# A decoder block on one core: the first down group in seven products, its stores and factors moved, and weights at the moving operands' place in every block

## The chip, the cores and the metric

The kernel runs on one core of a Trainium2 chip. A core has five engines that run at the same time and wait for each other through semaphores: TensorE (PE; its weight loads are shown apart as PEld), VectorE (DVE), ScalarE (ACT), GpSimd (POOL) and SyncE (SP). Transfers between the chip's memory and the core run on DMA queues, which SP and POOL fill here. The metric is the device time of one execution, in microseconds (us), median of three runs.

## The reference

What is computed is one decoder block on 512 tokens of width 2048: a norm, a combined input projection, two kinds of attention, an output projection with residual, then a feed-forward part and a last norm. The change touches the feed-forward part:

```python
    hn2 = rmsnorm(h, norm2_g[l])
    h = h + (jax.nn.silu(hn2 @ w_gate[l]) * (hn2 @ w_up[l])) @ w_down[l]
return rmsnorm(h, final_g)
```

`w_gate` and `w_up` are 2048 x 5632, `w_down` is 5632 x 2048, all float32. The result must have float32 quality.

## The kernel before

**Three matmuls for one.** A float32 operand is split in two parts, a high one (`h`, rounded to TensorE's fast format, by ACT) and a low one (`l`, the rest, by DVE). A product is then three matmuls, high by high, high by low, low by high: `mm` (lines 1238 to 1241). For the weights the split is made as the kernel runs: ACT writes `wh` (line 143), DVE writes `wl` (line 146), for 512 columns at a time, which the text calls a half product's weights; `Twin` (lines 166 and 170) does it for two sets of 256. A list of such jobs is worked off three ahead of TensorE, through five buffers each of `wh` and `wl`.

**A place for weights.** `wsplit(even)` takes the weights' columns in a padded tile from column 32 where `even` is true and from column 16 else. The moving operands (`ah`, `al`, the terms of `hn2`) always start at column 32. So `even` means that weights lie in the moving operands' place; the text calls such a job "placed".

**The feed-forward part.** The hidden width of 5632 is worked off in 44 blocks `f` of 128. A block's gate and up values are four products (two weights, two halves of the contraction) by two token halves. They are computed as seven products of sums (a Strassen scheme), P1 to P7, each of 2 half products of 12 matmuls with 256 columns, so a block has 168. The sums of weights are made by DVE in place in the loaded tile `raw` (`comb`, line 819; `prep`, line 843), or, in the order `ORDER1`, one of them by an accumulating load on POOL's queue (`fetch`, line 823). `ORDER0` is block 0's order, `ORDER1` that of block 1 and of blocks with f % 4 of 3 and 0 above 4, `ORDER` that of the others.

**The down product** takes four blocks at a time, a group. For groups 1 to 9 it, too, has seven products: `down7` works on 56 pairs (output block k, product name), each of 6 matmuls, sorted into a first single one ahead of the last product of block f = 8, 12, ..., then 27 twins of two behind it, and a last single one in the next block. Its moving operands are sums of the silu values, made by `hidden_terms`, and its results are staged by ACT and added to `kept_sums` in memory by accumulating DMA writes on POOL's queue (line 1161). Group 0 (blocks 0 to 3) has eight products: `down`, 16 jobs of 24 matmuls with weights of their own (`wdn`, tile `rawd`), interleaved with block 4's later products; its 16 results are stored plainly (line 1338), after zeros were stored where no result of it falls (line 1365). Group 10 is the kernel's end and not touched.

**The residual.** The feed-forward's input `hs` (16 tiles of 128 x 512) leaves the core to make room: `put_away` stores it through POOL's queue (line 1357), eight tiles from block 1 on, eight from block 2 on, and at the last one opens the pool in which group work has its tiles. It comes back in blocks 5, 6, 9, 10, 13, 14, 17, 18 (`add_residual`), scaled by `inv`.

**The factors.** `inv` and `r2` come from the second norm. In block 0 each is spread over 512 columns by four matmuls (`Spread`, line 279; each is two passes) and copied to a buffer by ACT (line 282).

**Order of work.** Each engine has one queue, in the order in which the program issues. `later(n, f)` puts a piece of work n half products further back in that order; it makes no engine wait by itself. SP's queue issues weight loads as buffers come free, five `raw` tiles of 512 KB. POOL's queue issues the fetches, the stores and the accumulating writes, with at most eight in flight.

Of the kernel before, what the change touches and what calls it, by code (L numbers as in the profile page):

```python
# [23 lines left out]
PH = 4  # L24
# [18 lines left out]
def plan():  # L43

    p = [("c", u) for u in range(8)]
    n = 0
    for name in ("ks", "kw", "vs", "vw"):
        for half in range(2):
            p.append(("in", name, 0, half))
            for _ in range(W1_AFTER[name][half]):  # L50
                p.append(("w1", n))
                n += 1
    for j in range(NH):
        if j == 4:
# [12 lines left out]
    return p  # L67
# [7 lines left out]
def block_kernel(ctx: ExitStack, tc: tile.TileContext, xt, wst, wdn, smalls, wg, w2c, bias, ident_in, out):  # L75
# [710 lines left out]

    dn_loads = deque((0, nb) for nb in range(KB))
    dn = {}

    def load_dn():  # L790
        if dn_loads:
            k = dn_loads.popleft()
            dn[k] = wp.tile([128, 512], F32, tag="rawd", name="rawd", bufs=2)
            sp.dma_start(dn[k], wdn[k[0], k[1]])

    fin = []
# [14 lines left out]
    def quad_jobs(f, names):  # L811
# [59 lines left out]
    def dn_job(p, nb):  # L871
        return Job(lambda: dn[p, nb], post=load_dn)

# [37 lines left out]
    for f in range(FB):  # L911
        qj = quad_jobs(f, order(f))
        p = f // PH - 1
        nb = 0
        for i, name in enumerate(order(f)):
            seq = sorted(((k, n) for k in range(8) for n in DTIME), key=lambda x: 7 * x[0] + DTIME[x[1]])
            if name == "P3" and f > PH and f % PH == 0:
                downs(p, seq[:1], True)
            sched.append(("q", f, name))
            jobs += qj[2 * i:2 * i + 2]  # L920
            if name == "P3" and f > PH and f % PH == 0:
# [13 lines left out]
    state["total"] = len(jobs)  # L935
    load_dn()
    load_dn()

# [8 lines left out]
    def close_attention():  # L947
# [16 lines left out]
        def close():  # L964
# [8 lines left out]
            for _ in range(2):  # L973
                ffn.tile([128, S], F32, tag="ft", name="ft", bufs=2)
            rest["hsp"] = ExitStack()
# [41 lines left out]
    def ft(name="ft"):  # L1017
        return ffn.tile([128, S], F32, tag="ft", name=name, bufs=2)

    sacc = ft("sacc")  # L1020
# [87 lines left out]
    banks["P5"] = ps.tile([128, 512], F32, tag="o", name="P5")  # L1108
    dbanks = {}
# [31 lines left out]
    def down7(p, k, name, wh, wl):  # L1141

        if not roles:
            seed = ps.tile([128, 512], F32, tag="misc", name="pd")
            pe.matmul(seed[:, :256], ones, sm[:, :1].to_broadcast([128, 256]), start=True, stop=True)
            roles.append((banks["P3"], banks["P4"], seed, dbanks[1]))
            roles.append((banks["P1"], banks["P5"], banks["P7"], banks["P6"]))
# [36 lines left out]
    def hidden_terms(f):  # L1184

        i = (f - 1) % 2
        x3 = st["x3"]
        hl = [[a[:, 12:16, :].rearrange("p t (i c) -> p t i c", c=256)[:, :, i, :] for a in (ah, al)],
              [a.rearrange("p (t i c) -> p t i c", i=2, c=256)[:, :, i, :] for a in x3]]

# [6 lines left out]
        if f % PH in (1, 2):  # L1197
            top = held[f - 1]
            t = st["pool"].tile([128, 1, 256], F32, tag="s2", name="t1", bufs=2)

            def s1():
                dve.tensor_tensor(t[:, 0, :], top[:, LO], top[:, HI], op=OP.subtract)
                hi(1, 2, 3, top[:, None, LO])

            def s2():
                lo(1, 2, 3, top[:, None, LO])
                hi(0, 2, 3, t)
# [15 lines left out]
        def s2():  # L1223
            dve.scalar_tensor_tensor(t24[:, 0, :], t3[:, 0, :], -1.0, top[:, LO], op0=OP.mult, op1=OP.subtract)
            lo(0, 0, 2, botv)
            hi(0, 3, 4, t3)

        def s3():
            dve.scalar_tensor_tensor(t24[:, 1, :], t24[:, 0, :], -1.0, bot[:, LO], op0=OP.mult, op1=OP.subtract)
            lo(0, 3, 4, t3)  # L1230
            hi(1, 0, 2, t24)
# [11 lines left out]
    def finish(f, g, u, c):  # L1243
        whole = u
        g, u = g[:, c], u[:, c]
        h, l = ah[:, 12 + f % PH, c], al[:, 12 + f % PH, c]
        wait = 0 if f == FB - 1 else 1 if f < 8 or f % PH else 2

# [17 lines left out]
        later(n, up)  # L1266
        if f < PH or f > FB - PH:
            later(n + 1, lambda: dve.scalar_tensor_tensor(l, u, -1.0, h.bitcast(F32), op0=OP.mult, op1=OP.subtract))
# [9 lines left out]
    def after(f, name):  # L1278
# [43 lines left out]

    def down(ph, nb):
        n = nb % 3
        if n not in dbanks:
            dbanks[n] = banks["P3"] if not n else (ps.tile([128, 512], F32, tag="t", name="pd", bufs=2) if n == 1 else
                                                ps.tile([128, 512], F32, tag="misc", name="pd"))
        p = dbanks[n]
        h, l = next_half()
        for c in (LO, HI):  # L1330
            for i in range(PH):
                mm(p[:, c], h[:, 128 * i:128 * i + 128], l[:, 128 * i:128 * i + 128], ah[:, 12 + i, c],
                   al[:, 12 + i, c], i == 0, i == PH - 1)

        def add():
            t = st["pool"].tile([128, 2, 256], F32, tag="stga", name="stg", bufs=3)
            act.activation(t, p.rearrange("p (t c) -> p t c", c=256), AF.Copy, scale=1.0 if nb < 8 else -1.0)
            pool_e.dma_start(mem_at(nb), t)

        later(1, add)  # L1340

    def mem_at(nb):
# [13 lines left out]
    def put_away(nb):  # L1356
        pool_e.dma_start(kept_hs[nb], hs[:, nb, :])
        if nb == KB - 1:
            rest["hsp"].close()
            st["dnp"] = ExitStack()  # L1360
            pool = st["pool"] = st["dnp"].enter_context(tc.tile_pool(name="dnp", bufs=1))
            zero = pool.tile([128, 256], F32, tag="s2", name="zero", bufs=2)
            pool_e.memset(zero, 0.0)
            for k in range(8):
                pool_e.dma_start(kept_sums[k][:, 2, :], zero)
            st["x3"] = [placed(pool, 3 * S, at, name="x3" + x) for x, at in (("h", MH), ("l", ML))]
            for name, x, n in (("P2", 0, 0), ("P3", 0, 1), ("P5", 0, 2), ("P7", 0, 3), ("P6", 1, 0), ("P4", 1, 1), ("P1", 1, 2)):
                parts[name] = tuple((b[:, S * n:S * n + S] if x else a[:, 12 + n, :]).rearrange("p (i c) -> p i c", c=256)
# [10 lines left out]
    for kind, a, b in sched:  # L1379
        if kind == "d":  # L1380
            down(a, b)
            continue
        if kind == "s":
# [19 lines left out]
        if PH < f <= FB - PH and name == order(f)[2]:  # L1403
            for i, s in enumerate(hidden_terms(f)):
# [7 lines left out]
        if f == 0:  # L1412
# [5 lines left out]
            if name == "P6":  # L1418
                st["inv"] = st["inv"]()
                act.activation(st["rs2"].rs[:, 7, :1], ones[:, :1], AF.Silu)  # L1420
# [163 lines left out]
```

## Time and profile before

| | us |
|---|---|
| median of 3 runs | 2143.21 |
| lowest, highest | 2142.64, 2144.26 |
| the profiled execution | 2147.43 |
| its span | 2145.6 |
| granted TensorE clock, mean over it | 0.997 |

The profiled execution is one run with the hardware profiler on. Its span goes from the first to the last instruction; 1.8 us lie around it. The page's rows give busy time and counts by engine, then groups of instructions by line. Matmuls overlap, so their rows' durations (277 ns) are not their distance; the distance is read from the start times, or from a stretch's length by the number of matmuls that start in it. The feed-forward part's products run from 836.0 to 2085.6 us of the span.

### The profile page before, as it was taken

The page shows a single profiled execution, that of the slowest core. Times are in us where ns is not written, and L with a number is a line of the kernel's source. Part 1 is how long each engine was busy: PE and PEld are TensorE (multiplying, and loading weights), DVE is VectorE, ACT ScalarE, POOL GpSimd, SP SyncE. Part 2 cuts the span into 40 slices and gives each one's busy share as a digit, 9 for nine tenths or more (in the row PEclk, how much of TensorE's full clock was granted, in tenths as well). Part 3 has the DMA queues.
Part 4 walks back from the last instruction along what each step waited for, and adds up shares of the span by engine and source line. Part 5 has one row for each costly group of instructions (what it writes and reads, how often), then busy time and mean ns, then how long its engine had stood idle before and what let it go on. Part 6 is the DMA issues. An engine that isn't in the chain of part 4 may idle for free.

```text
span 2145.6 us, 41296 instructions
## 1 busy us (share of the span) xinstructions
PE 2128.1 (99%) x15346; PEld 1988.0 (93%) x15346; DVE 1629.4 (76%) x3460; ACT 1241.6 (58%) x2973; POOL 321.9 (15%) x378
## 2 busy tenths in 40 slices
PE   9999999999999999999999999999999999999997
PEld 7888888888888888999999999999999999999997
DVE  6755656366657678856989898898989898988885
ACT  6544444344445256444675858585767667675856
POOL 0000000000000001211131313131212213030323
PEclk9999999999999999999999999999999999999998
DMA  7442222322234334545596969775766758594982
GB/s 237 147 141 81 82 82 69 101 81 72 65 106 155 99 99 128 177 153 148 145 230 142 213 154 210 171 188 139 184 161 158 184 141 187 139 216 118 208 245 89
DMA packets 124347, 313.67 MB, mean 146 GB/s; under 512 B 13424, under 2 KB 35568, under 8 KB 124144
## 3 DMA queue, kind: packets, MB, share of 16 engines
q1 hardware_dynamic: 77104, 236.49, 34.9%
q0 software_dynamic: 46896, 74.47, 19.6%
q8 instruction: 120, 1.97, 0.4%
q14 instruction: 83, 0.68, 0.1%
q10 hardware_dynamic: 144, 0.07, 0.0%
HBM read 245.96 MB, written 65.01 MB: 145 GB/s over the span
## 4 chain that ended last, share of the span: by engine, by line
PE 96%; DMA 1%; DVE 1%; ACT 1%; issue 0%; SPq 0%; POOL 0%; DVEq 0%; ACTq 0%; POOLq 0%
PE P L1241 17%; PE P L1240 17%; PE P L1239 17%; PE pp L197 7%; PE pp L199 7%; PE pp L198 7%; PE pab L199 3%; PE pab L197 3%; PE pab L198 3%; PE pd L1239 2%; PE pd L1241 2%; PE pd L1240 2%; DMA raw<-in_wst_dram 1%; PE pt L568 1%; PE po L198 1%; PE pl L198 1%
## 5 line engine op out<-in xcount | busy, mean ns | idle before, releaser
L143 ACT ACTIVATE wh<-raw 128x512 fp32r<-128x512 f32 x888 | 532.7, 625 | 295.0 <-DVE raw L819 113.6
L146 DVE TENSOR_TENSOR wl<-raw,wh 128x512 fp32r<-128x512 f32 x888 | 599.3, 686 | 111.0 <-ACT wh L143 106.9
L1241 PE MATMUL P<-ah,wl 128*128 128x256 f32 x1536 | 426.1, 277 | 0.1
L1239 PE MATMUL P<-ah,wh 128*128 128x256 f32 x1536 | 425.2, 277 | 0.0
L1240 PE MATMUL P<-al,wh 128*128 128x256 f32 x1536 | 425.1, 277 | 0.0
L1241 PEld LDWEIGHTS P<-ah,wl 128*128 128x128 f32 x1536 | 288.3, 188 | 1.3 <-DVE wl L146 1.1
L1240 PEld LDWEIGHTS P<-al,wh 128*128 128x128 f32 x1536 | 288.4, 188 | 0.0
L1239 PEld LDWEIGHTS P<-ah,wh 128*128 128x128 f32 x1536 | 288.2, 188 | 0.0
L197 PE MATMUL pp<-ah,wh 128*128 128x512 f32 x640 | 260.5, 407 | 0.0
L199 PE MATMUL pp<-ah,wl 128*128 128x512 f32 x640 | 251.0, 392 | 0.0
L198 PE MATMUL pp<-al,wh 128*128 128x512 f32 x640 | 250.2, 391 | 0.0
L1161 POOL DMA_DIRECT2D sums<-stg x216 | 188.1, 927 | 312.0 <-ACT P L1155 150.0
L819 DVE TENSOR_TENSOR raw<-raw 128x512 f32<-128x512 f32 x270 | 185.7, 688 | 5.6 <-DMA raw<-in_wst_dram 2.0
L170 DVE TENSOR_TENSOR wl<-raw,wh 128x256 fp32r<-128x256 f32 x432 | 167.9, 420 | 27.3 <-ACT wh L166 25.8
L166 ACT ACTIVATE wh<-raw 128x256 fp32r<-128x256 f32 x432 | 159.2, 409 | 4.6 <-DVE raw L898 4.6
L199 PEld LDWEIGHTS pp<-ah,wl 128*128 128x128 f32 x640 | 120.2, 188 | 28.2 <-DVE wl L146 0.4
L197 PEld LDWEIGHTS pp<-ah,wh 128*128 128x128 f32 x640 | 120.5, 188 | 20.0 <-DVE tmp L369 0.5
L198 PEld LDWEIGHTS pp<-al,wh 128*128 128x128 f32 x640 | 120.6, 189 | 19.5
L555 ACT ACTIVATE e<-e,st 128x512 f32<-128x512 f32 (+1 forms) x96 | 53.7, 560 | 124.3 <-DVE st L549 124.3
L707 POOL TENSOR_TENSOR acc<-acc,osq 128x512 f32<-128x512 f32 x14 | 18.1, 1294 | 580.3 <-ACT osq L706 580.3
L1155 ACT ACTIVATE stg<-P 128x256 f32<-128x256 f32 x252 | 95.6, 381 | 12.7 <-PE P L1241 3.3
L197 PE MATMUL pab<-ah,wh 128*128 128x512 f32 x256 | 100.3, 392 | 0.0
(335 smaller groups left out, 5545.0 us busy)
## 6 DMA issues: line engine op xcount, KB each, us to landing
raw<-in_wst_dram SPq DMA_DIRECT2D x382, 512.0 KB, 4.2
sums<-stg POOLq DMA_DIRECT2D x160, 256.0 KB, 6.7
raw<-in_wst_dram POOLq DMA_DIRECT2D x42, 256.0 KB, 4.5
sums<-stg POOLq DMA_DIRECT2D x72, 128.0 KB, 6.3
bias<-in_bias_dram SPq DMA_DIRECT2D x16, 320.0 KB, 3.0
xc<-in_xt_dram SPq DMA_DIRECT2D x16, 256.0 KB, 3.5
rawd<-in_wdn_dram SPq DMA_DIRECT2D x16, 256.0 KB, 2.8
hs<-in_xt_dram SPq DMA_DIRECT2D x16, 256.0 KB, 5.7
```

Of the source, the lines that this page charges most:

```text
L143: act.activation(self.h, self.src(), AF.Copy)
L146: dve.tensor_tensor(self.l, self.src(), self.h.bitcast(F32), op=OP.subtract)
L166: act.activation(h, src(), AF.Copy)
L170: dve.tensor_tensor(l, src(), h.bitcast(F32), op=OP.subtract)
L197: pe.matmul(o, wh, mh, start=start, stop=False)
L198: pe.matmul(o, wh, ml, start=False, stop=False)
L199: pe.matmul(o, wl, mh, start=False, stop=stop)
L819: return lambda: dve.tensor_tensor(o(), o(), x(), op=OP.add)
L1161: return lambda s=sums[x]: pool_e.dma_start(kept_sums[k][:, q:q + n, :], s, accum_op=OP.add)
L1239: pe.matmul(o, wh, mh, start=start, stop=False, skip_group_check=True)
L1240: pe.matmul(o, wh, ml, start=False, stop=False, skip_group_check=True)
L1241: pe.matmul(o, wl, mh, start=False, stop=stop, skip_group_check=True)
```

## The change

It changes four things.

1. Group 0 is computed by seven products, too: its `downs` are scheduled in block 4 as the other groups' are in theirs, `down`, `dn_job`, `load_dn` and the separate weight loads go, and `hidden_terms` also runs for blocks 1 to 4. Its results are written to `kept_sums` plainly instead of accumulating, and the zeros are no longer stored. Blocks 0 to 3 keep their silu products (`held`) in two new buffers `early`, one `ft` buffer and one of the group pool. As the group pool is not open in blocks 1 and 2, the operand of P1 moves from the pool's tile to `ah`, that of P7 the other way, and a scratch tile becomes the idle PSUM bank of P3.
2. Block 1 makes its sums on DVE as `ORDER` blocks do (in the order of products of `ORDER1`); its two fetches on POOL's queue go. All 16 residual stores are issued from block 1's P1 on, in steps of 8/5 half products.
3. In block 0, `r2`'s four matmuls and copy come first; `inv`'s copy is put five half products further back.
4. The first job of every block but block 0 is placed (before: odd blocks and block 2), and so are two of the 27 twins of each group, n = 19 and n = 37, beside the first single one, which was placed already.

```diff
-        if f > PH and f % PH == 0:
+        if f and f % PH == 0:
             p += [("dn", f // PH - 1, k) for k in range(8)]
...
-            elif order(f) == ORDER1:
+            elif order(f) == ORDER1 and f > 1:
...
-        r["P1", 0].even = f == 2 or f % 2 == 1
+        r["P1", 0].even = f > 0
...
-            if name == "P3" and f > PH and f % PH == 0:
+            if name == "P3" and f and f % PH == 0:
                 for n in range(1, len(seq) - 1, 2):
-                    downs(p, seq[n:n + 2])
-            if name == "P1" and f > PH + 1 and f % PH == 1:
+                    downs(p, seq[n:n + 2], n in (19, 37))
+            if name == "P1" and f > PH and f % PH == 1:
                 downs(p, seq[-1:])
-            if f == PH and i > 2:
-                for _ in range(4):
-                    if nb < KB:
-                        sched.append(("d", p, nb))
-                        jobs.append(dn_job(p, nb))
-                        nb += 1
...
-    AWAY = {(1, "P1"): (0, 8, 0), (2, "P1"): (8, 8, 0)}
+    AWAY = {(1, "P1"): (0, 16, 0)}
...
         def add(x, q, n):
-            return lambda s=sums[x]: pool_e.dma_start(kept_sums[k][:, q:q + n, :], s, accum_op=OP.add)
+            how = {"accum_op": OP.add} if p else {}
+            return lambda s=sums[x]: pool_e.dma_start(kept_sums[k][:, q:q + n, :], s, **how)
...
-            t = st["pool"].tile([128, 1, 256], F32, tag="s2", name="t1", bufs=2)
+            t = banks["P3"][:, None, :256]
...
-        wait = 0 if f == FB - 1 else 1 if f < 8 or f % PH else 2
+        wait = 0 if f == FB - 1 else 1 if f < PH or f % PH else 2
...
-            if PH <= f <= FB - PH:
+            if f <= FB - PH:
                 dve.scalar_tensor_tensor(u, u, -1.0, g, op0=OP.mult, op1=OP.mult)
                 held[f] = whole
...
-                st["u"] = (st["pool"].tile([128, S], F32, tag="hf", name="hf", bufs=4)
-                           if PH <= f <= FB - PH else ft())
+                st["u"] = (ft() if f == 2 or f > FB - PH else early() if f == 1 else
+                           st["pool"].tile([128, S], F32, tag="hf", name="hf", bufs=4))
...
-            zero = pool.tile([128, 256], F32, tag="s2", name="zero", bufs=2)
-            pool_e.memset(zero, 0.0)
-            for k in range(8):
-                pool_e.dma_start(kept_sums[k][:, 2, :], zero)
...
             for i in range(n):
-                later(at + i, lambda nb=first + i: put_away(nb))
+                later(at + 8 * i // 5, lambda nb=first + i: put_away(nb))
...
             if name == "P6":
-                st["inv"] = st["inv"]()
                 act.activation(st["rs2"].rs[:, 7, :1], ones[:, :1], AF.Silu)
                 st["r2"] = st["r2"](tag="t", bufs=2)
-                st["u"] = ft()
+                inv, pinv = st["inv"].r, st["inv"](False)
+                st["inv"] = inv
+                later(5, lambda: act.activation(inv, pinv, AF.Copy))
+                st["u"] = early()
```

More of the change, by code (lines that the diff above doesn't have):

```diff
@@ L920, in block_kernel @@
             jobs += qj[2 * i:2 * i + 2]
-            if name == "P3" and f > PH and f % PH == 0:
+            if name == "P3" and f and f % PH == 0:
                 for n in range(1, len(seq) - 1, 2):
-                    downs(p, seq[n:n + 2])
-            if name == "P1" and f > PH + 1 and f % PH == 1:
+                    downs(p, seq[n:n + 2], n in (19, 37))
+            if name == "P1" and f > PH and f % PH == 1:
                 downs(p, seq[-1:])
-            if f == PH and i > 2:
-                for _ in range(4):
-                    if nb < KB:
-                        sched.append(("d", p, nb))
-                        jobs.append(dn_job(p, nb))
-                        nb += 1
     for nb in range(KB):
@@ L972, in close @@
                                    for x, at in (("h", MH), ("l", ML)))
-            for _ in range(2):
-                ffn.tile([128, S], F32, tag="ft", name="ft", bufs=2)
+            for tag in ("ft", "early"):
+                for _ in range(2):
+                    ffn.tile([128, S], F32, tag=tag, name=tag, bufs=2)
             rest["hsp"] = ExitStack()
@@ L1018, in ft, with early @@
         return ffn.tile([128, S], F32, tag="ft", name=name, bufs=2)
+    def early():
+        return ffn.tile([128, S], F32, tag="early", name="early", bufs=2)
     sacc = ft("sacc")
@@ L1145, in down7 @@
             pe.matmul(seed[:, :256], ones, sm[:, :1].to_broadcast([128, 256]), start=True, stop=True)
-            roles.append((banks["P3"], banks["P4"], seed, dbanks[1]))
+            roles.append((banks["P3"], banks["P4"], seed, ps.tile([128, 512], F32, tag="t", name="pd", bufs=2)))
             roles.append((banks["P1"], banks["P5"], banks["P7"], banks["P6"]))
@@ L1186, in hidden_terms @@
         i = (f - 1) % 2
-        x3 = st["x3"]
-        hl = [[a[:, 12:16, :].rearrange("p t (i c) -> p t i c", c=256)[:, :, i, :] for a in (ah, al)],
-              [a.rearrange("p (t i c) -> p t i c", i=2, c=256)[:, :, i, :] for a in x3]]
+        hl = [[a[:, 12:16, :].rearrange("p t (i c) -> p t i c", c=256)[:, :, i, :] for a in (ah, al)]]
+        if "x3" in st:
+            hl.append([a.rearrange("p (t i c) -> p t i c", i=2, c=256)[:, :, i, :] for a in st["x3"]])
         def hi(w, a, b, src):
@@ L1225, in s2 @@
             lo(0, 0, 2, botv)
-            hi(0, 3, 4, t3)
+            hi(1, 2, 3, t3)
         def s3():
             dve.scalar_tensor_tensor(t24[:, 1, :], t24[:, 0, :], -1.0, bot[:, LO], op0=OP.mult, op1=OP.subtract)
-            lo(0, 3, 4, t3)
+            lo(1, 2, 3, t3)
             hi(1, 0, 2, t24)
@@ L1321, in after @@
             finish(f, g, u, HI if f == FB - 1 else slice(0, 512))
[L1323 to L1340, printed above, removed]
     def mem_at(nb):
@@ L1379, in block_kernel @@
     for kind, a, b in sched:
-        if kind == "d":
-            down(a, b)
-            continue
         if kind == "s":
@@ L1402, in block_kernel @@
                 later(n, lambda nb=8 * (f - FB + 3) + n: bring_back(nb))
-        if PH < f <= FB - PH and name == order(f)[2]:
+        if 0 < f <= FB - PH and name == order(f)[2]:
             for i, s in enumerate(hidden_terms(f)):
```

21 lines of the change are left out of this document (4 added, 17 removed).

## The prediction

> **What bounds the kernel now.** I read the page first, then the waits of TensorE's weight loads, then stretches of the feed-forward part, then single rows where one stretch was slower than its neighbour.
>
> ```profile
> span 2145.6 us, 41296 instructions
> PE 2128.1 (99%) x15346; PEld 1988.0 (93%) x15346; DVE 1629.4 (76%) x3460; ACT 1241.6 (58%) x2973; POOL 321.9 (15%) x378
> PE 96%; DMA 1%; DVE 1%; ACT 1%; issue 0%; SPq 0%; POOL 0%; DVEq 0%; ACTq 0%; POOLq 0%
> ```
>
> TensorE is the chain. So time is (number of matmuls) x (distance from one start to the next) plus the few places where it stands. The waits, and stretches of blocks f (columns: length, then busy us and count of PE, PEld, DVE, ACT, POOL, then PEclk, DMA share, GB/s):
>
> ```profile
> PEld P L1239 <- ACT wh L143: 2.2, 1, 2.2
> PEld P L1241 <- DVE wl L146: 2.1, 6, 1.0
> PEld P L1239 <- DVE ft L1302: 1.2, 1, 1.2
> ...
> 1013.45 0.19 PEld L1241 LDWEIGHTS P<-ah,wl 128*128 128x128 f32 x1 [0.21 <-DVE wl L146]
> ...
> 861.16:878.84 17.68, 17.68 (x158) 17.68 (x157) 14.16 (x25) 8.81 (x17) 9.33 (x16) 1.00 0.66 199
> 880.28:890.96 10.68, 7.84 (x51) 7.33 (x50) 7.24 (x14) 4.27 (x9) 3.63 (x8) 0.84 0.68 265
> 903.68:905.12 1.44, 1.44 (x15) 1.44 (x13) 1.41 (x4) 0.00 (x0) 0.00 (x0) 1.00 0.00 0
> 905.12:923.49 18.37, 18.37 (x158) 18.37 (x157) 15.88 (x28) 10.59 (x21) 0.00 (x0) 1.00 0.40 116
> 859.61:988.50 128.89, 126.05 (x1056) 125.54 (x1057) 85.82 (x145) 59.98 (x115) 24.63 (x40) 0.99 0.50 164
> 988.50:989.93 1.43, 1.43 (x14) 1.43 (x13) 1.11 (x2) 1.12 (x2) 0.00 (x0) 1.00 0.84 239
> 989.93:1007.61 17.68, 17.68 (x158) 17.68 (x157) 12.16 (x23) 9.40 (x20) 1.95 (x2) 1.00 0.53 157
> 1046.57:1063.05 16.48, 16.48 (x147) 16.48 (x146) 15.60 (x30) 9.40 (x20) 1.72 (x2) 1.00 0.48 113
> 1063.60:1105.00 41.40, 41.40 (x354) 41.40 (x353) 35.07 (x87) 36.00 (x113) 18.45 (x22) 1.00 0.94 214
> 1186.15:1221.59 35.44, 35.44 (x301) 35.44 (x302) 29.93 (x74) 32.29 (x101) 18.30 (x22) 1.00 0.99 222
> 1990.90:2026.30 35.40, 35.40 (x301) 35.40 (x301) 29.89 (x74) 32.32 (x101) 18.38 (x22) 1.00 1.01 222
> ```
>
> The reader should see **two gaits**. Thirteen half products (156 matmuls; the row's 158 counts those that reach over the edges) take 17.68 us in blocks 1 and 5, 113.3 ns each, but 18.37 us in block 3, 117.8 ns each, at the same clock and with no wait. TensorE walks 4.5 ns slower per matmul from a bubble on. What ends the slow gait: block 5's first half product, whose weights lie in the moving operands' place, takes 1.43 us for 12 (119.2 each) and the rest is fast. Block 3's such job (1.44) did not do it, so the reset is likely, not sure. The slow gait holds for all of 905.12 to 988.50 (block 4 has no such job), and in the down groups at 1063.6, 1186.2 and 1990.9 (35.4 us / 300 = 118).
>
> Block 2 also stands still: 10.68 us for 48 matmuls, which are 5.44 at 113.3, so 5.24 lost, with the clock at 0.84. Its cause:
>
> ```profile
> 843.96 10.75 SPq L115 DMA_DIRECT2D raw<-in_wst_dram  x4
> ...
> 838.32 1.44 POOL L1357 DMA_DIRECT2D res<-hs  x2
> 866.09 0.89 POOL L823 DMA_DIRECT2D raw<-in_wst_dram  x1 [26.32 <-issue]
> 867.91 4.26 POOL L1357 DMA_DIRECT2D res<-hs  x7
> 883.13 0.63 ACT L143 ACTIVATE wh<-raw 128x512 fp32r<-128x512 f32 x1 [6.60 <-DMA raw<-in_wst_dram]
> ...
> res<-hs POOLq DMA_DIRECT2D x14, 256.0 KB, 7.7
> raw<-in_wst_dram SPq DMA_DIRECT2D x4, 512.0 KB, 9.7
> ```
>
> Two residual stores leave at 838; the third stands on POOL behind block 1's accumulating fetch, which waits until 866. So 14 stores meet block 2's four weight loads, which land after 9.7 us instead of the page's median:
>
> ```profile
> raw<-in_wst_dram SPq DMA_DIRECT2D x382, 512.0 KB, 4.2
> ```
>
> **Part by part.**
>
> *Seven products for group 0.* Before: 16 x 8 x 3 = 384 matmuls; after: 8 x 7 x 2 x 3 = 336. 48 fewer, all from slow ground: 48 x 117.8 = 5.65 us. The seed matmul comes here from group 1:
>
> ```profile
> 1062.77 0.28 PE L1241 MATMUL P<-ah,wl 128*128 128x256 f32 x1
> 1062.89 0.60 PE L1145 MATMUL pd<-sm,ones 128*128 128x256 f32 x2
> 1063.13 0.47 PE L1239 MATMUL P<-x3h,wh 128*128 128x256 f32 x1
> 1063.44 0.28 PE L1240 MATMUL P<-x3l,wh 128*128 128x256 f32 x1
> ```
>
> It costs 0.24 + (0.31 - 0.12) = 0.43 us and, as group 1 shows, leaves the slow gait behind it.
>
> *Stores and fetch.* Block 1 loses its two fetches, so on POOL nothing stands before the 16 stores but a free place in its ring: they will run from 838 on, back to back, whatever the larger spacing in the program says. At 7.4 us for eight in flight (14 of them took 7.7) they end near 838 + 2 x 7.7 = 853. They then meet the four weight loads issued from 843.96 to 854.71, which are block 1's, instead of block 2's. With 9.7 us to landing an issue at 847 lands near 857, about when the weights of block 1's second product are split; TensorE needs those only at 858.5 + 1.44 + 1.36 = 861.3. Bounds 0 to the 5.24 of block 2; I take 0. The zeros (a memset, eight 128 KB stores) go; nobody waited for them. Group 0's sums become plain writes, behind which POOL has nothing urgent, and its sixteen 256 KB weight loads become eight of 512 KB on SP, in the main ring as in the other groups. The two early buffers, the PSUM bank as scratch and the swapped places of P1 and P7 move operands only: nothing.
>
> *Entry factors.* The end of block 0:
>
> ```profile
> 854.94 0.60 ACT L282 ACTIVATE r<-prb 128x512 f32<-128x512 f32 x1 [1.37 <-PE prb L279]
> 855.54 1.28 ACT L1420 ACT_TABLE_LOAD   x1
> 856.94 0.58 ACT L282 ACTIVATE r<-prb 128x512 f32<-128x512 f32 x1
> 857.42 2.18 ACT L143 ACTIVATE wh<-raw 128x512 fp32r<-128x512 f32 x4
> ...
> 858.08 0.69 DVE L146 TENSOR_TENSOR wl<-raw,wh 128x512 fp32r<-128x512 f32 x1 [2.33 <-ACT wh L143]
> 859.13 0.42 DVE L1302 TENSOR_TENSOR ft<-P,r 128x256 f32<-128x256 f32 x1
> ```
>
> ACT stood 1.37 us for the first copy, then loaded a table, and split, DVE and TensorE's 1.2 us wait followed. After, the table load comes first and fits into the 1.37; the second factor's copy follows the first four matmuls (854.94), so the wh of 857.42 comes near 855.5, and L1302 near 858.3, where block 0's matmuls end. Bounds 0 to 1.2; I take 1.1. The copy moved five half products later (0.60 of ACT, which is busy 8.81 of 17.68 there) is hidden by that idle time; uncovered it would cost its 0.60. What is late next is DVE.
>
> *DVE's added work.* Operations start 0.60 us apart:
>
> ```profile
> 862.25 0.69 DVE L146 TENSOR_TENSOR wl<-raw,wh 128x512 fp32r<-128x512 f32 x1
> 862.85 0.69 DVE L819 TENSOR_TENSOR raw<-raw 128x512 f32<-128x512 f32 x1
> ```
>
> Block 1: one 512-wide fewer, three 256-wide more, under 0.5 us against the 3.5 that DVE idles in its stretch: nothing. Block 4 has two 512-wide adds more than the like block 8, whose stretch before the down work (1046.57 to 1063.05) is 15.60 of 16.48 busy; 1.2 more overfills it by 0.3. Bounds 0 and 1.2; I take 0.3. ACT (9.40 there) covers its own new copies.
>
> *The place in every block.* New jobs: blocks 2 (had one), 4, 6, ... 42, and two twins in each of ten down groups. After block 4 there are 19 + 18 jobs x 12 x (120.0 - 113.3) = 3.0 us of cost. Gain there: group 1 loses the seed and with it 351 slow matmuls, 1.6 + 0.4; groups 2 and 9 get fast again after the first new twin, each (300 - 96) x 4.5 ns = 0.9. Of the six waits for DVE's wl, four are of the kind shown at 1013.45 (block 6, and alike in 10, 14, 18, where a residual is added); a slower job ahead gives DVE 0.08 us more room: 0.3. Net +1.1.
>
> [...]
>
> *Sum.* Blocks 1 to 3: 3 x (1.44 + 17.68) = 57.36. Block 4: 1.43 + 11 x 1.36 (17.68 / 13) = 16.39; seed 0.43; first twin 0.72; P3 and nine twins slow, 132 x 117.8 = 15.55; placed twin 1.43; eight twins 10.88; placed 1.44; eight 10.88; together 57.72, and 0.68 for the last product in block 5. 115.8 against 128.89: 13.1 less, and 12.8 with DVE's 0.3. Plus 1.1 before and 1.1 behind: **15.0 us**.
>
> The span of 2145.6 would become 2130.6. The profiled execution took 2147.43, 4.22 above the median 2143.21. If that is an even surcharge the new median is 2128.2; if it is part of the waits that go, 2132.4. Most of the gain is counts and gaits, not waits: I take 2129.2.
>
> **Rivals.**
> A. *The wait moves*: stores meet block 1's loads. For it: the full ring from 838, with four loads in it. Against: the 4 us between a late landing and TensorE's need. Price 5.24 and up to 0.75 of slow gait (168 x 4.5 ns): 6.0, so 2128.2 + 6.0 to 2132.4 + 6.0, middle **2136**.
> B. *Slower: a placed job in a fast stream leaves it slow.* Place: the 20 new block jobs (156 matmuls behind each, 14.0 us) and 20 twins (96 behind each, 8.6). All flipped: 22.6 against a gain of 14, **2152**. It turns the sign when over 62% flip. For it: block 3's job, which left slow ground slow. Against: block 5's, and block 1's own, both with a fast stretch behind them.
> C. *The change does not do what it says: the place has no effect*, gaits come from waits alone. Then no cost of 3.0, no resets; blocks 1 to 4 stay on block 0's slow ground: 1008 x 117.8 + 0.43 = 119.2, 9.7 less; with 1.1 and group 1's 0.4: 11.2, **2132**. [...] Against: block 1 went fast behind its placed job.
> D. *The first down group waits for DVE throughout*: 1.2 at each of two places and slow gait for the whole group (330 x 4.5 ns = 1.5): 3.6 worse, **2133**.
>
> **How the numbers follow.** Forecast 0.60, A 0.15, B 0.10, C 0.05, D 0.10. Low end: the four waits of blocks 6 to 18 go (0.3 each, and 120 slow matmuls each): 4 x 0.8 = 3.2 below 2128.2, 2125. High end 2138.4, A on the upper median. No change means within 0.2% (4.3 us), which a measurement can tell: only B partly flipped ends there. Faster 0.87, same 0.05, slower 0.08.
>
> **What would show it.** Right: no wait on in_wst_dram in block 2, clock 1.00 there; blocks 1 to 3 at 19.1 us; PE 48 matmuls fewer; the wait on ft gone; slow gait only in block 0, behind the seed, and behind the DVE waits. Wrong: a wait in block 1 (A), 117.8 behind placed jobs (B), slow gait throughout blocks 1 to 4 (C), wl waits through block 4 (D).

## The result and the profile after

| | before | after |
|---|---|---|
| median of 4 runs, us | 2142.93 | 2132.07 |
| lowest, highest | 2141.80, 2144.26 | 2130.74, 2134.17 |
| the profiled execution | 2147.43 | 2134.17 |
| its span | 2145.6 | 2132.1 |

The ratio is 0.9946 (95% interval 0.9929 to 0.9962): 10.9 us fewer on the medians, 13.5 on the two profiled spans. The forecast was 2129.2, 14.0 fewer.

From the page of the changed kernel, the span, the engines and the chain:

```profile
span 2132.1 us, 41370 instructions
PE 2119.3 (99%) x15298; PEld 1980.7 (93%) x15298; DVE 1654.0 (78%) x3540; ACT 1259.9 (59%) x3059; POOL 316.9 (15%) x375
PE 99%; DVE 0%; issue 0%; ACT 0%; DVEq 0%
```

TensorE has 48 matmuls fewer and is now the whole chain. The waits of its weight loads in the feed-forward part (here L1222 to L1224 are the lines of `mm`):

```profile
PEld P L1222 <- DVE ft L1285: 0.2, 1, 0.2
...
PEld pd L1222 <- ACT pd L1137: 0.2, 1, 0.2
PEld P L1224 <- DVE wl L146: 0.2, 1, 0.2
```

Block 2's wait for `wh` of 2.2 us is gone, the entry's wait for `ft` is 0.2 instead of 1.2, and of six waits for `wl` one is listed. The wait on ACT's `pd` is in a down group, in block 32. Then the stretches (length, busy us and count of PE, PEld, DVE, ACT, POOL, PEclk, DMA share, GB/s). The first two are block 2, the next four block 4, the seventh blocks 1 to 4, the last from block 5 to the start of block 43:

```profile
877.72:879.15 1.43, 1.43 (x14) 1.43 (x13) 1.40 (x3) 0.00 (x0) 0.00 (x0) 1.00 0.37 149
879.15:896.84 17.69, 17.69 (x159) 17.69 (x157) 15.66 (x29) 10.52 (x22) 0.00 (x0) 1.00 0.40 120
923.12:931.59 8.47, 8.47 (x74) 8.47 (x73) 8.44 (x17) 5.48 (x12) 0.00 (x0) 1.00 0.41 126
934.15:949.70 15.55, 15.55 (x135) 15.55 (x134) 14.31 (x38) 13.36 (x42) 3.23 (x6) 1.00 0.66 199
949.70:951.13 1.43, 1.43 (x15) 1.43 (x13) 1.02 (x3) 1.23 (x5) 0.54 (x1) 1.00 0.41 126
951.13:962.01 10.88, 10.88 (x99) 10.88 (x97) 9.24 (x23) 10.15 (x33) 3.59 (x7) 1.00 0.81 245
858.50:974.33 115.83, 115.83 (x1005) 115.61 (x1005) 105.93 (x217) 79.31 (x200) 11.57 (x22) 1.00 0.47 144
974.33:2052.46 1078.13, 1078.13 (x9416) 1077.20 (x9415) 949.11 (x1926) 735.26 (x1863) 249.71 (x282) 1.00 0.72 175
```

Block 2 takes 1.43 + 17.69 us at clock 1.00, with nothing lost. Block 4 shows both gaits: 8.47 us for 72 matmuls (117.6 ns each) and 15.55 for 132 (117.8), then the placed twin at 949.70 and behind it 10.88 for 96 (113.3). Blocks 1 to 4 take 115.83 us against 128.89. The last row has its counterpart in the kernel before, over the same blocks:

```profile
988.50:2065.16 1076.66, 1076.40 (x9413) 1074.97 (x9411) 945.61 (x1920) 735.54 (x1860) 248.78 (x280) 1.00 0.73 175
```

The row of after holds the last product of group 0, 6 matmuls or 0.68 us, which moved into block 5. So 1077.45 against 1076.66: behind block 4 the changed kernel is 0.8 us slower.

How the stores went, from the timeline of POOL and the view of transfers between 838 and 857 us of after:

```profile
838.16 4.62 POOL L1321 DMA_DIRECT2D res<-hs  x8
844.37 4.17 POOL L1321 DMA_DIRECT2D res<-hs  x7 [1.60 <-DMA res<-hs]
848.77 0.54 POOL L1321 DMA_DIRECT2D res<-hs  x1 [0.22 <-issue]
...
res<-hs POOLq DMA_DIRECT2D x16, 256.0 KB, 6.4
raw<-in_wst_dram SPq DMA_DIRECT2D x4, 512.0 KB, 6.3
```

Eight go out back to back, the ninth after 1.60 us of waiting until a store has landed; the last is issued at 848.77 and takes 8.7 us, so it lands near 857.5. The four weight loads beside them land after 6.3 us instead of 4.2, and TensorE waits for none.

And the end of block 0, from the timeline of ACT:

```profile
853.42 1.28 ACT L1376 ACT_TABLE_LOAD   x1
...
854.83 0.58 ACT L282 ACTIVATE r<-prb 128x512 f32<-128x512 f32 x1
855.30 1.14 ACT L143 ACTIVATE wh<-raw 128x512 fp32r<-128x512 f32 x2
```

The table comes first, and `wh` follows at 855.30 instead of 857.42.

### The profile page after: what moved, and what is told of

It is laid out like the page before. It is cut to its first block, busy times and chain, and to the rows that moved or that the text cites. A ratio compares the mean times of both kernels' runs of the same rounds, so it can differ in the third digit from the quotient of the medians.

```text
span 2132.1 us, 41370 instructions
## 1 busy us (share of the span) xinstructions
PE 2119.3 (99%) x15298; PEld 1980.7 (93%) x15298; DVE 1654.0 (78%) x3540; ACT 1259.9 (59%) x3059; POOL 316.9 (15%) x375
## 4 chain that ended last, share of the span: by engine, by line
PE 99%; DVE 0%; issue 0%; ACT 0%; DVEq 0%
PE P L1224 18%; PE P L1223 18%; PE P L1222 18%; PE pp L197 7%; PE pp L199 7%; PE pp L198 7%; PE pab L198 3%; PE pab L199 3%; PE pab L197 3%; PE pd L1222 1%; PE pd L1224 1%; PE pd L1223 1%; PE pt L568 1%; PE pl L198 1%; PE po L198 1%; PE po L197 1%
## 5 line engine op out<-in xcount | busy, mean ns | idle before, releaser
L1224 PE MATMUL P<-ah,wl 128*128 128x256 f32 x1616 | 448.1, 277 | 0.0
L1222 PE MATMUL P<-ah,wh 128*128 128x256 f32 x1616 | 447.6, 277 | 0.0
L1223 PE MATMUL P<-al,wh 128*128 128x256 f32 x1616 | 447.3, 277 | 0.0
L1224 PEld LDWEIGHTS P<-ah,wl 128*128 128x128 f32 x1616 | 303.5, 188 | 0.7 <-DVE wl L146 0.2
L1222 PEld LDWEIGHTS P<-ah,wh 128*128 128x128 f32 x1616 | 303.5, 188 | 0.0
L1223 PEld LDWEIGHTS P<-al,wh 128*128 128x128 f32 x1616 | 303.5, 188 | 0.0
L1144 POOL DMA_DIRECT2D sums<-stg x240 | 201.0, 889 | 429.1 <-ACT P L1137 150.9
L170 DVE TENSOR_TENSOR wl<-raw,wh 128x256 fp32r<-128x256 f32 x480 | 186.5, 419 | 30.0 <-ACT wh L166 28.1
L166 ACT ACTIVATE wh<-raw 128x256 fp32r<-128x256 f32 x480 | 176.6, 409 | 4.8 <-DVE raw L886 4.8
L1137 ACT ACTIVATE stg<-P 128x256 f32<-128x256 f32 x280 | 106.7, 382 | 14.2 <-PE P L1224 2.7
```

The source lines that it names most:

```text
L166: act.activation(h, src(), AF.Copy)
L170: dve.tensor_tensor(l, src(), h.bitcast(F32), op=OP.subtract)
L1222: pe.matmul(o, wh, mh, start=start, stop=False, skip_group_check=True)
L1223: pe.matmul(o, wh, ml, start=False, stop=False, skip_group_check=True)
L1224: pe.matmul(o, wl, mh, start=False, stop=stop, skip_group_check=True)
```

## The experiments

The theory behind all of them: the time is the number of matmuls times the gait, plus a few waits; a bubble can leave the slow gait behind it, and a run of placed matmuls ends it. The counts of slow and fast matmuls below are made from the start times in each trace, job by job: a job is slow where the median distance between its matmuls is 116 to 119 ns. All kernels compute the whole reference.

### What the gait of the kernel before is worth

The kernel before, unchanged, profiled once more.

> The kernel before, unchanged, profiled once more. The first profiled execution took 2147.43 us, 4.2 above the median. Theory A (its surcharge sits in the wait of block 2): here block 2's loss, 5.24 us in the first profile, is 1 to 4 us, and the span is shorter by as much. Theory B (the surcharge is even, from profiling): the loss is again 5 us and the span again 2145 to 2146.

It took 2142.54 us (one run), with a span of 2140.8, 4.8 less than the profile of the prediction. Its stretches for block 2's stall, block 3's last thirteen half products, blocks 1 to 4:

```profile
879.94:890.18 10.24, 6.80 (x50) 5.83 (x49) 7.31 (x15) 4.22 (x9) 3.11 (x7) 1.00 0.66 263
...
903.85:921.54 17.69, 17.69 (x158) 17.69 (x157) 15.80 (x27) 10.48 (x21) 0.00 (x0) 1.00 0.41 120
859.28:984.10 124.82, 121.38 (x1056) 120.41 (x1057) 85.44 (x145) 59.64 (x115) 24.72 (x40) 1.00 0.52 169
```

The stall is there again, 10.24 - 5.44 = 4.8 us, so neither theory holds. What differs is what it left: here the stream came out fast (17.69 against 18.37), and 816 slow matmuls fewer in blocks 1 to 4, at 4.5 ns, are 3.7 us of the 4.1 between 128.89 and 124.82. So most of the difference between the two profiles is the gait behind the stall.

### Does the place set the gait?

No feed-forward job placed (`even` false everywhere), and every job placed:

```diff
-        r["P1", 0].even = f > 0
+        r["P1", 0].even = False
...
-                downs(p, seq[:1], True)
+                downs(p, seq[:1])
...
-                    downs(p, seq[n:n + 2], n in (19, 37))
+                    downs(p, seq[n:n + 2])
```

```diff
-        r["P1", 0].even = f > 0
+        for j in r.values():
+            j.even = True
...
-                    downs(p, seq[n:n + 2], n in (19, 37))
+                    downs(p, seq[n:n + 2], True)
...
-                downs(p, seq[-1:])
+                downs(p, seq[-1:], True)
```

> The changed kernel with no placed job in the feed-forward part. Theory A (a placed job ends the slow gait, nothing else does): all 10752 matmuls stay at 117.8 ns; the 8424 that run at 113.3 in the changed kernel cost 4.5 ns more each, 37.9 us, the 816 placed ones 2.2 ns less, 1.8 us, and some waits for DVE go: 2132.1 + 35 = about 2167 us. Theory B (the gait comes from waits alone and the place has no effect): block 1 runs fast without it, and the time is 2127 to 2132.

> The changed kernel with every job of the feed-forward blocks and down groups placed. Theory A (a placed job is itself slower, 120.0 ns a matmul): 8424 matmuls get 6.7 ns and 1512 get 2.2 ns more, 60 us, less some waits for DVE: about 2190 us. [...]

None placed: 2168.36 us, ratio to before 1.0104 (1.0078 to 1.0129). All placed: 2191.26, 1.0210 (1.0184 to 1.0236). The same thirteen half products of block 2, without and with places everywhere, then blocks 5 to 42 of the second:

```profile
879.39:897.74 18.35, 18.35 (x158) 18.35 (x157) 15.11 (x29) 10.39 (x22) 0.00 (x0) 1.00 0.40 116
```

```profile
879.99:898.71 18.72, 18.72 (x158) 18.72 (x157) 14.88 (x28) 10.09 (x22) 0.00 (x0) 1.00 0.39 113
979.06:2108.74 1129.68, 1129.68 (x9417) 1129.68 (x9415) 951.96 (x1927) 739.35 (x1863) 249.69 (x282) 1.00 0.71 168
```

18.35 / 156 is 117.6 ns, 18.72 / 156 is 120.0, against 113.4 in the changed kernel, at the same clock and without a wait. Without places the stream goes slow in block 0 and never recovers: of its 10752 feed-forward matmuls no job runs at 113, and blocks 5 to 42 take 1108.76 us, with PE busy throughout, against the 1078.13 of the changed kernel. With TensorE slower, DVE is in time: in the trace without places the only wait of a weight load of `mm` is the 0.2 us for `ft`. So the place acts twice: a placed matmul costs 120, and a run of them brings 113 back. Rival C is refuted. With every job placed PE is busy for the whole of the two stretches above, 18.72 and 1129.68 us, so no wait is recorded in them; yet where the weights lie moves the time by 59 us (2191.26 against 2132.07). What makes a placed matmul slower is not shown. Nor is it shown that the shared place does it and not column 32 by itself: the moving operands start at column 32 in every run.

### The fetch

The changed kernel with block 1's two fetches kept:

```diff
-            elif order(f) == ORDER1 and f > 1:
+            elif order(f) == ORDER1:
```

> The changed kernel with block 1's sums made as before, so that its two accumulating fetches stand again on POOL between the residual stores. Theory A (the stores behind the fetch, meeting block 2's weight loads, made block 2's wait): the first stores leave at 838, the others after 866, TensorE loses 3 to 5 us in block 2 and runs slow until block 3's placed job (0.6): 2135 to 2138 us. Theory B (the wait went because the other edits of the change gave room): no wait in block 2, 2132 or a little less, as DVE has two adds less.

2136.98 us over 7 runs, 0.9959 (0.9947 to 0.9971). Its block 2:

```profile
878.24:901.04 22.80, 21.02 (x170) 20.07 (x169) 18.00 (x34) 12.01 (x25) 0.00 (x0) 1.00 0.59 205
```

22.80 against 19.12 is 3.7 us more, and PE was busy for 21.02 of the 22.80: the wait is back, and behind it the slow gait until block 3's placed job. Its cause, from the timelines of POOL and ACT and the view of transfers between 864 and 886 us:

```profile
838.29 1.45 POOL L1321 DMA_DIRECT2D res<-hs  x2
864.10 0.89 POOL L814 DMA_DIRECT2D raw<-in_wst_dram  x1 [24.36 <-issue]
...
865.94 4.12 POOL L1321 DMA_DIRECT2D res<-hs  x7
...
880.49 0.63 ACT L143 ACTIVATE wh<-raw 128x512 fp32r<-128x512 f32 x1 [5.71 <-DMA raw<-in_wst_dram]
...
raw<-in_wst_dram SPq DMA_DIRECT2D x4, 512.0 KB, 9.5
```

Two stores leave at 838, the others stand behind the fetches until 866, and the weight loads that they meet land after 9.5 us. Allowing the stores from block 1 on isn't enough; what holds them is the fetch ahead of them on POOL. By run times alone this kernel can't be told from the changed one (0.9946, 0.9929 to 0.9962): it is the trace that shows the wait.

### Each part alone

The four parts of the change one by one. First the kernel before with the stores and the fetch of part 2, with the factors of part 3, and with the places of part 4:

```diff
-            elif order(f) == ORDER1:
+            elif order(f) == ORDER1 and f > 1:
...
-    AWAY = {(1, "P1"): (0, 8, 0), (2, "P1"): (8, 8, 0)}
+    AWAY = {(1, "P1"): (0, 16, 0)}
...
-                later(at + i, lambda nb=first + i: put_away(nb))
+                later(at + 8 * i // 5, lambda nb=first + i: put_away(nb))
```

```diff
-                st["inv"] = st["inv"]()
...
+                inv, pinv = st["inv"].r, st["inv"](False)
+                st["inv"] = inv
+                later(5, lambda: act.activation(inv, pinv, AF.Copy))
```

```diff
-        r["P1", 0].even = f == 2 or f % 2 == 1
+        r["P1", 0].even = f > 0
...
-                    downs(p, seq[n:n + 2])
+                    downs(p, seq[n:n + 2], n in (19, 37))
```

The fourth is the changed kernel with these three undone, which leaves the seven products of group 0.

> The kernel before with part 2's stores and fetches alone: all 16 residual stores from block 1 on, block 1's sums on DVE. Theory A (the stores run from 838 on, meet block 1's loads and cost nothing there): no wait on in_wst_dram in block 2, clock 1.00 in it; 5 us fewer where the stream behind block 2's wait would have been fast anyway, up to 9 where it would have been slow: 2135 to 2139 us. Theory B (the wait only moves to block 1): a wait of 3 to 6 us on wh in block 1, 2141 to 2145 us, no gain that can be measured.

> The kernel before with part 3's factors alone. Theory A (the copy order is what held block 1's entry): the wait on ft of 1.2 us falls to 0.2, all else as before: about 1.1 us fewer, 2142 us, too little to be told from the runs' own spread, so it is to be read from the trace: block 0's last matmul to block 1's first. Theory B (DVE is late there for its own work): the wait stays at 1 us or more.

> The kernel before with part 4's places alone. Block 2's wait stays (5 us). Theory A (a placed job ends the slow gait and does not start it): blocks 3 and 4 come fast whatever gait the wait leaves, the second half of each down group gets fast at the placed twin; the placed jobs cost 20 + 18 times 12 x 6.7 ns = 3.0 us: 0 to 4 us fewer than before, 2139 to 2144, and a smaller spread from run to run. Theory B (a placed job in a fast stream leaves it slow): slower, by up to 22 us if every one did.

> The changed kernel with block 1's fetches, the stores' spacing, the factors and the places as before: the seven products of the first down group alone. Theory A (48 fewer matmuls, at the gait of block 4, which nothing resets there): 5.2 to 5.7 us fewer, minus the seed's 0.4: 2137 to 2140 us. Theory B (DVE's added sums eat it): waits on wl in block 4 of over 1 us in all and a gain under 3 us, 2142 or more.

| alone | median, us | lowest, highest | ratio to before (95%) |
|---|---|---|---|
| before, 29 runs | 2146.56 | 2141.53, 2152.60 | |
| stores and fetch | 2139.18 | 2137.75, 2143.58 | 0.9972 (0.9961 to 0.9982) |
| factors | 2145.00 | 2141.47, 2148.66 | 0.9993 (0.9982 to 1.0004) |
| places | 2144.45 | 2142.82, 2147.21 | 0.9991 (0.9982 to 1.0000) |
| seven products | 2136.64 | 2136.16, 2139.77 | 0.9960 (0.9946 to 0.9975) |

*Stores.* Block 2 of this run:

```profile
879.15:898.27 19.12, 19.12 (x171) 19.12 (x169) 16.96 (x29) 10.60 (x21) 0.00 (x0) 1.00 0.39 118
```

No wait and no slow gait, as theory A had it; rival A of the prediction, a late load in block 1, is refuted. But a part of the price did move to block 1's entry, where the wait on `ft` grew from 1.2 to 1.9 us. DVE's new sum for block 1 stands there ahead of `ft`:

```profile
858.39 0.69 DVE L819 TENSOR_TENSOR raw<-raw 128x512 f32<-128x512 f32 x1
...
859.45 0.42 DVE L1302 TENSOR_TENSOR ft<-P,r 128x256 f32<-128x256 f32 x1
...
PEld P L1239 <- DVE ft L1302: 1.9, 1, 1.9
```

In the whole change the wait is 0.2 us: there the reordered factors take this 0.7 us away with the rest.

*Factors.* The wait on `ft` is not in the list of waits any more, and block 1 begins at 857.96. But the profile shows how little that can be worth by itself:

```profile
857.96:877.77 19.81, 19.81 (x170) 19.81 (x169) 16.46 (x29) 10.06 (x19) 9.33 (x16) 1.00 0.65 201
```

Block 1's placed job did not end the slow gait this time, and block 1 took 19.81 instead of 19.12: 0.7 of the 1.2 us is lost again.

*Places*, from block 5 to block 43:

```profile
984.90:2064.01 1079.11, 1078.45 (x9412) 1077.02 (x9411) 946.12 (x1920) 734.85 (x1860) 247.74 (x279) 1.00 0.73 175
```

2.45 us more than the 1076.66 of before: 444 more placed matmuls at 6.7 ns are 3.0, and 1140 slow ones instead of 1356 give back 1.0. Over the runs it is not slower (at most 0.2% faster); block 3 and 4 came out fast. None of the placed jobs of 12 matmuls made a fast stream slow: rival B is refuted.

*Seven products.* The gain is 8.6 us by the ratio, more than theory A's 5. Its rows for block 4, group 1's products, and blocks 5 to 42:

```profile
922.24:979.89 57.65, 57.60 (x502) 57.35 (x501) 51.94 (x119) 45.98 (x132) 11.78 (x22) 1.00 0.60 183
...
979.89:2054.36 1074.47, 1073.93 (x9416) 1072.82 (x9415) 949.05 (x1926) 735.79 (x1863) 248.38 (x282) 1.00 0.73 176
1055.70:1095.13 39.43, 39.43 (x350) 39.43 (x349) 34.93 (x87) 35.86 (x113) 18.33 (x22) 1.00 0.97 224
```

The expectation forgot group 1. Once the seed is in block 4, group 1 runs fast without any new place: 39.43 us for 348 matmuls is 113.3 each, where it was 118 before. Behind block 4 this kernel is 1076.66 - (1074.47 - 0.68) = 2.9 us faster than before, and the new places have no part in it. Block 4 had luck besides: in this profile the stream was slow ahead of the seed and came out fast behind it, the only one of twelve seeds that left it fast, so block 4 took 57.65 us without a placed twin.

### The places in the changed kernel, and better ones

All four on one chip: the changed kernel; the same with the old places; with the old places and new ones at known spots; and that with one twin per group:

```diff
-        r["P1", 0].even = f > 0
+        r["P1", 0].even = f == 2 or f % 2 == 1
...
-                    downs(p, seq[n:n + 2], n in (19, 37))
+                    downs(p, seq[n:n + 2])
```

```diff
-        r["P1", 0].even = f > 0
+        r["P1", 0].even = f in (0, 2) or f % 2 == 1
+        r["P6", 1].even = f in (4, 6, 10, 14, 18)
...
-                    downs(p, seq[n:n + 2], n in (19, 37))
+                    downs(p, seq[n:n + 2])
```

The last one has `n == 9` in place of `n in (19, 37)`.

> The changed kernel with part 4's places as before (odd blocks, block 2, the first single pair of each group). Theory A (behind block 4 the added places only cost: the group that they were to make fast is fast already, because the seed moved): 38 jobs x 12 x 6.7 ns = 3.0 us come back, at most 1 of it lost to slower stretches: 2 to 4 us faster than the changed kernel, and from block 5 to the last block about 1074.5 us, as with the seven products alone. Theory B (the prediction's: they give back 1.1 us more than they cost): 1 us slower than the changed kernel.

> As the run before, and a place where a stream goes slow at a known spot: the second P6 job in blocks 4, 6, 10, 14, 18 (right behind the wait for DVE's wl there) and block 0's first job. Theory A (one placed job right behind the bubble ends the slow gait): blocks 6, 10, 14, 18 lose 108 slow matmuls each, 0.41 us net, block 4 0.25, block 0 0.3: about 2 us faster than the run before. Theory B (a reset needs more, or the slower job moves the wait elsewhere): no difference of 1 us or more.

> As the run before, and twin n = 9 of each group placed, just behind the place where groups sometimes wait for DVE. Theory A (waits in groups come in one to four groups of ten, each costs 300 slow matmuls): the cost is 10 x 12 x 6.7 ns = 0.8 us, the gain 250 x 4.5 ns = 1.1 us for each group that waits: within 1 us of the run before on the median, with a smaller spread. Theory B (a slower job in a group with DVE full brings more waits, as four groups showed against one): slower by over 1 us.

> The changed kernel itself, beside the three above on the same chip: 2131 to 2134 us. Theory A (the waits in four groups come with the places): some of them again in its trace. Theory B (they come by chance): other groups, or none.

| | median, us | lowest, highest | ratio to before (95%) | profiled span | slow matmuls in it |
|---|---|---|---|---|---|
| before, 11 runs | 2144.20 | 2140.93, 2151.01 | | | |
| changed | 2132.62 | 2131.78, 2133.92 | 0.9947 (0.9934 to 0.9961) | 2130.3 | 1368 |
| old places | 2135.01 | 2130.05, 2137.68 | 0.9957 (0.9941 to 0.9973) | 2129.2 | 1440 |
| and known spots | 2133.52 | 2130.34, 2135.49 | 0.9949 (0.9934 to 0.9964) | 2133.6 | 2364 |
| and a twin per group | 2127.78 | 2126.46, 2130.68 | 0.9925 (0.9911 to 0.9939) | 2124.1 | 180 |

From block 5 to block 43, one row each in the order of the last four:

```profile
973.38:2050.65 1077.27, 1077.21 (x9417) 1076.41 (x9415) 949.85 (x1926) 735.03 (x1863) 248.08 (x281) 1.00 0.73 176
```

```profile
974.72:2049.51 1074.79, 1074.26 (x9416) 1072.95 (x9415) 949.18 (x1926) 735.37 (x1863) 249.53 (x282) 1.00 0.73 176
```

```profile
974.41:2053.99 1079.58, 1079.42 (x9416) 1077.95 (x9415) 949.34 (x1926) 736.11 (x1863) 247.63 (x281) 1.00 0.74 175
```

```profile
973.10:2044.45 1071.35, 1071.32 (x9417) 1070.37 (x9415) 949.21 (x1926) 735.89 (x1863) 247.88 (x281) 1.00 0.73 177
```

*Old places.* In the profiles theory A holds: 2.5 us less than the changed kernel beside it (1077.27), 3.3 less than its first profile (1078.13). In the times it does not: the median is 2.4 us higher, the intervals overlap, and the runs lie 7.6 us apart instead of 2.1. So the new places cost about what was counted, and with them the few runs lay closer together; whether they gain or lose on the median stays open.

*Known spots.* In blocks 6, 10, 14 and 18 the stream went on fast behind P6's wait, so nothing was left to reset there; in block 4 it went slow, and the second P6 job did not end it. (In the next kernel's trace it did so in blocks 4, 6 and 14.) The profiled run has 924 slow matmuls more than the old places' (4.2 us; the spans differ by 4.4): four groups went slow, one behind a wait for DVE's `wl` (block 28), one behind a wait for ACT's `pd` (24), one behind a gap of 0.06 us (40), one with no gap (32), and twice the next placed job did not reset them. The 2 us cannot be told from this scatter.

*A twin per group.* Expected within 1 us of the run before, it is 5.7 below it and 4.8 below the changed kernel; all five of its runs lie below the changed kernel's lowest, though the two intervals touch. The trace has 180 slow matmuls left. But it does not show the twin at work in a later group: two groups (blocks 24 and 40) had a gap of 0.04 and 0.06 us ahead of the twin n = 5, and both went on fast; only block 4's twin ended a slow stretch. That this version is the fastest measured is shown; why its groups come out fast is not.

*The changed kernel again.* Groups went slow in blocks 24, 32 and 40, three of the four of its first profile (24, 28, 32, 40). With the old places they did so in 28 and 40, in the kernel before in 8, 12 and 40. The spots come again, as theory A says, but blocks 28 and 40 went slow with the old places, too, and in the run with block 1's fetches kept, which has the new places, no group behind block 4 did. So the spots are largely the kernel's own and which of them falls is partly chance; that the new places bring them is not shown.

## Why the prediction was nearly right, point by point

The time alone does not decide: rivals C (2132) and D (2133) lie nearer to the measured 2132.07 than the forecast of 2129.2. The rows and the runs with other places do.

**What bounds the kernel: right.** Gaits and counts explain the differences between profiles: 924 slow matmuls between two of the last four are 4.2 us, their spans differ by 4.4.

**Seven products: right in kind, sized short.** 48 matmuls went and the seed was paid in block 4. The part alone was worth 8.6 us (5.4 to 11.6) against 5.65 less 0.43. The prediction booked the fast group 1 (2.0) under the places; it came with the seed's move, and the fast gait behind the seed in block 4 may have added to it.

**Stores and fetch: right.** Block 2's loss is gone and the collision with block 1's loads cost nothing, as taken. That DVE's added sum costs nothing holds only together with the factors; with the stores alone it made 0.7 us. The loads landed after 6.3 us, not the 9.7 feared. The one correction is that part of the price was gait: the second profile of before shows the same stall without the slow blocks behind it.

**Entry factors: right.** The wait fell from 1.2 to 0.2. By run times the part alone can't be told from nothing.

**DVE in block 4: wait right, consequence missed.** DVE was late for one P6 job in the block's first half, just ahead of the row of 923.12:

```profile
921.83 0.19 PEld L1224 LDWEIGHTS P<-ah,wl 128*128 128x128 f32 x1 [0.17 <-DVE wl L146]
```

TensorE stood for 0.2 us, inside the bounds, but the stream was slow from there to the seed, eight jobs of 12 matmuls or 0.4 us that the sum did not have. Rival D is refuted: behind the seed the group's rows (934.15 to 962.01) show PE busy throughout, and this is the one listed wait for `wl`. Blocks 1 to 4 took 115.83; the sum had 57.36 + 57.72 + 0.3 = 115.38.

**Places: the step that failed.** The prediction gave them +1.1 behind block 4; 0.8 was lost there instead. The cost of 3.0 was right (444 more placed matmuls; 2.45 net in the kernel before). Of the gains, group 1's 2.0 belonged to the seed, so the places' own sum was -0.9 from the start. Slow matmuls did go where the sum expected it: 912 in blocks 8, 12 and 40 (4.1 us), though group 2 (block 12) did not wait at all this time and only block 40 was reset by its twin. What the sum left out is 672 slow matmuls (3.0 us) in blocks 10, 15, 24, 28 and 32, which were fast in the profile of before. In block 15 the first placed job failed to reset, in block 24 the twin n = 19. The groups of blocks 24, 28 and 32 went slow behind gaps of at most 0.2 us; the profile names a cause for one, in block 32: ACT's copy to `pd`, held up by DVE's sum `s`:

```profile
1747.84 0.42 ACT L166 ACTIVATE wh<-s 128x256 fp32r<-128x256 f32 x1 [1.13 <-DVE s L883]
...
1748.42 0.38 ACT L1137 ACTIVATE pd<-P 128x256 f32<-128x256 f32 x1
...
1748.85 0.19 PEld L1222 LDWEIGHTS pd<-x3h,wh 128*128 128x128 f32 x1 [0.20 <-ACT pd L1137]
```

Waits other than those of the kernel before were priced in block 4 alone. And a reset is a chance, as the prediction said, but its sum took it as sure.

**From the span to the median.** On the two spans 13.5 us went, against the sum's 15.0: 1.9 short behind block 4 and 0.45 in block 4, against 0.8 gained behind 2052.46, outside all steps (79.6 us to the end of the span, 80.4 before). The other 1.4 of the 2.9 us is the conversion. Between 2128.2 (an even surcharge) and 2132.4 (a surcharge in what goes) the prediction took 2129.2. Neither end was right: the first profiled run of before lies 4.5 us above its median, that of the changed kernel still 2.1 above its own, so about half of the surcharge went. That 2132.07 lies next to 2132.4 is luck, as the sum under it was 1.5 too large. The repeat of before, on another chip, lay 3.4 us below the median of the ten runs there. One profiled run is one draw, and a surcharge read from it was no firm term.

## What to carry to other kernels

Where TensorE is never idle, measure the distance between matmuls stretch by stretch: two gaits 4% apart (113.3 and 117.8 ns) can hide under 99% busy, and a short wait can leave several times its length in the stretch behind it: in the kernel before 0.32 us for ACT's `pd` at 1186.14, then 35.44 us for 300 matmuls, 1.45 more than at 113.3. Before an edit is credited with a gain, ask whether another edit of the same change removes the cause first. And take a second profile of the same kernel before a difference of a few us is explained: here one stall left either gait.

## What the runs showed of the hardware that was not expected

- A bubble leaves either gait. Six profiles have a stall in block 2; behind it the stream was slow (117.8 ns) in five and fast (113.3) in one. Three times in the twelve traces a stream went slow with no wait beside it, with single distances of 123 ns at most; the other way round nothing but a placed run or a bubble did it, and with none placed the slow gait lasted to the end.
- A run of 12 placed matmuls reached in the slow gait, with no gap inside it, ended it 80 times out of 97, and 347 reached in the fast gait all left it fast, counted over the twelve traces with both kinds of jobs. Ten more, all at block 1's entry, stood 305 ns or more behind the matmul ahead, with one distance of 221 to 226 inside, and all ten ended it; the two entries without that gap (the factors alone, the fetch kept) did not. With such a gap of 311 and no place the stream stayed slow (the run with none placed). So part of block 1's reset may be the bubble's, which the runs do not separate. The failures show a pattern of single distances up to 124 or 125 ns; the others stay at 121 or below.
- During block 2's stall TensorE's clock fell in the first profile (0.84 over the stretch, with matmuls 213 ns apart) and stayed at 1.00 in the next, with nearly the same loss (5.2 and 4.8 us).
- The runs of the kernel before lie 11 us apart (29 runs), those of the changed kernel 3.4 and 2.1 (4 and 5 runs). Only the profiled ones show their gait; that the rest of the scatter is the same thing is likely, not shown.
